# A two-layer decoder kernel: two masks leave the matmul engine

## The chip, the cores and the metric

One core of one Trainium2 chip runs the whole program. The metric is the time on the device of one execution in microseconds (us), the median of several runs. TensorE is called PE here, VectorE DVE, ScalarE ACT, GpSimd POOL, and SyncE, which issues most of the transfers, SP.

## The reference, cut to what matters

The sequence has 512 positions and the model 1024 channels. Two layers follow each other, each a token mixer and a gated MLP with a short causal convolution. The two mixers are what the change touches:

```python
# layer 0: stick-breaking attention, 16 heads of width 64, blocks of 128 queries
z = einsum('bqhd,bshd->bhqs', qb, k)              # qb holds the factor 1/8
strict = key_pos[None, :] < t[:, None]
log_keep = where(strict, log_sigmoid(-z), 0.0)
suffix = cumsum(log_keep, axis=3, reverse=True) - log_keep
a = where(strict, exp(log_sigmoid(z) + suffix), 0.0)

# layer 1: 16 heads of width 128 over one shared latent; the 128 keys of each query are chosen by an indexer
_, sel = top_k(isc, topk)                          # isc is NEG above the diagonal
logits = einsum('bqhd,bqkd->bqhk', qb, kg) * scale + bias(t - sel, head)
logits = where(valid, logits, NEG)                 # NEG = -1e30
p = softmax(logits)
```

In layer 0 a query sees only the keys before it, and its weight at key s is sigmoid(z[s]) times the product of sigmoid(-z) over the keys between s and t. In layer 1 the bias depends on the distance from query to key and on the head.

## The kernel before, in words

Activations lie transposed, 128 channels by 512 positions. Every dense product is made of three matmuls of rounded parts (`mm3`, lines 248 to 251): a matrix and its operand are each split in a high part (ACT, line 209 for weights) and a remainder (DVE, line 217). Weights come as chunks of 128x1024 fp32 through a pool `raws` of six buffers (line 126); `fetch` (191) keeps their loads, all on SP's queue, one chunk ahead of the splits in the program, and the queue itself runs ahead as far as buffers are free. The order of the instructions is written out by hand (`manual_schedule`): each engine executes its instructions in the order of the program text.

**Layer 0's attention** (`stick_layer`, lines 496 to 969). Each head has four query tiles j = 0 to 3 with (j+1)*128 keys. `scores` (846) makes z in PSUM by two matmuls (852, 853). A third one (854) multiplies an identity by the 128x128 matrix `strict_b`, which holds -1e30 on and above the diagonal, and adds it to the last 128 columns. ACT then writes m = sigmoid(-z/8) (861) and a = sigmoid(z/8) (862): masked places give m = 1 and a = 0. DVE runs a product over m from the right in place (866, `tensor_tensor_scan` with multiply and bypass) and multiplies a by the result shifted by one (867). PE transposes a (882), and `weighted` (894) multiplies it with the values (904). Between these, projections of later heads fill PE (`fill`, 837).

**Layer 1's attention** (`dsa_layer`, lines 1049 to 1498). The indexer leaves `maskb`, bf16, 0 or -1e30, 128x1280: the four query tiles side by side at columns LOFF = 0, 128, 384, 768. For a head h and a tile j, `logits` (1337) makes z by three matmuls (1343 to 1345) and a fourth one (1346), identity times the tile's part of `maskb`, that adds the mask. `softmax` (1348) scales z by the query's norm and adds the head's bias on DVE (1354), and takes the negative maximum (1356); `expo` (1358) is ACT's exponential with the row sums (1361). `transposed` (1365) turns the result on PE (1372) and copies it out of PSUM. There are two PSUM buffers for z, so a tile's logits wait until DVE has read the tile two before it. The bias lies in DRAM as one row per head (`rb`); `load_bias` (1325) loads it with a step of one element per partition, which makes a 128x512 table that all four tiles read backwards, into one of two buffers `th`.

Head 0's four tiles are made ahead of the loop (1436 to 1440). The loop (1448) over h then mixes the logits and softmax of head n = h+1 with the transposes of head h, the values of a pair of heads (1383, 1393), and steps of the last query projections and of the output projection (`fill`, 1319, whose `events` also hold the weight splits). At the end of an iteration it calls `load_bias(n + 1)` (1487), whose table is first read in the next iteration.

The lines that matter, with the line numbers of the profile:

Of the kernel before, what the change touches and what calls it, by code (L numbers as in the profile page):

```python
# [9 lines left out]
F32 = mybir.dt.float32  # L10
F32R = mybir.dt.float32r
BF = mybir.dt.bfloat16
AF = mybir.ActivationFunctionType
OP = mybir.AluOpType
# [4 lines left out]
D = 1024  # L19
S = 512  # L20
P = 128
KT = D // P
QT = S // P
# [4 lines left out]
HEADS = 16  # L28
# [4 lines left out]
NEG = -1e30  # L33
# [5 lines left out]
LATE_STEPS = [2, 3, 2, 3, 3, 3, 3, 3, 3, 3, 5, 5, 5, 5, 5, 8]  # L39
AHEAD = 2  # L40
FETCH = 1
IDXFILL = [1, 1, 1, 0, 1, 1, 1, 1]

TRP = [[(0, 0)], [(1, 0), (3, 384)], [(2, 0)]]
TRW = [512, 512, 256]
LOFF = [0, 128, 384, 768]
LW = 1280
TRO = [0, 512, 1024]

C_ID, C_STRICT, C_CAUSAL = 0, 128, 256  # L50
C_W = 384

S_ADAB, S_NM, S_NF, S_CW, S_CB = 0, 48, 56, 64, 64 + 132
S_L = 64 + 132 + 44
# [64 lines left out]
def kernel_body(ctx, tc, xT, wst, cst, smalls, crow, ccol, relb, onehot, outT):  # L119
    nc = tc.nc  # L120
# [16 lines left out]
    cons = cpool.tile([P, C_W], F32, name="cons")  # L137
    ident = cons[:, C_ID:C_ID + P]
    ident_b = cpool.tile([P, P], BF, name="ident_b")
    strict_b = cpool.tile([P, P], BF, name="strict_b")  # L140
    ones_mean = cpool.tile([P, P], F32, name="ones_mean")
    dve.memset(ones_mean, 1.0 / D)
    ecols = cpool.tile([P, 3], F32, name="ecols")
# [352 lines left out]
    def stick_layer(l):  # L496
        with ExitStack() as st:
# [233 lines left out]
                first_part(i, KT - 2)  # L731
            lo_part(KT - 1)
            dve.tensor_copy(ident_b, ident)
            dve.tensor_copy(strict_b, cons[:, C_STRICT:C_STRICT + P])
            V, O, QK, A_ = {}, {}, {}, {}
            kz = [[ap.tile([P, S], F32R, name=f"kz{b}{e}", bufs=1) for e in range(2)] for b in range(2)]
            for b in range(2):
# [108 lines left out]
            def scores(i, j):  # L846
                p, e = i // 2, i % 2
                q, kd, kl = QK[p][e], QK[p][2 + e], QK[p][4 + e]
                ns = (j + 1) * P
                z = ptile([P, S], "z", "z")  # L850
                qs = slice(j * P, ns)
                pe.matmul(z[:, :ns], lhsT=q[:, qs], rhs=kd[:, :ns], start=True, stop=False)
                pe.matmul(z[:, :ns], lhsT=q[:, qs], rhs=kl[:, :ns], start=False, stop=False)
                pe.matmul(z[:, qs], lhsT=ident_b, rhs=strict_b, start=False, stop=True)
                if j == 0:
                    A_[i] = ap.tile([P, LW], F32, name="a")
                a = A_[i][:, LOFF[j]:LOFF[j] + ns]

                def gates():
                    m = ap.tile([P, S], F32, name="m", bufs=2)  # L860
                    act.activation(m[:, :ns], z[:, :ns], AF.Sigmoid, scale=-0.125)
                    act.activation(a, z[:, :ns], AF.Sigmoid, scale=0.125)

                    def weights():
                        rev = m[:, :ns][:, ::-1]
                        dve.tensor_tensor_scan(rev, rev, rev, 1.0, OP.mult, OP.bypass)
                        dve.tensor_mul(a[:, :ns - 1], a[:, :ns - 1], m[:, 1:ns])

                    later(0.4, weights)

                later(0.2, gates)
                tick(0.1 * j + 0.15)
# [176 lines left out]
    def dsa_layer(l, first, man):  # L1049
        with ExitStack() as st:  # L1050
# [233 lines left out]
            with ExitStack() as sa:  # L1284
# [34 lines left out]
                def fill(n):  # L1319
                    for _ in range(n):  # L1320
                        next(filler, None)
                        if events:
                            events.pop(0)()

                def load_bias(h):
                    th = ths[h] = ap.tile([P, S], F32, name="th", bufs=2)
                    ov = rb[h:h + 1, 0:1]
                    nc.sync.dma_start(th, bass.AP(tensor=ov.tensor, offset=ov.offset, ap=[[1, P], [1, S]]))

                def begin(h):  # L1330
                    L = ap.tile([P, LW], F32, name="L")
# [5 lines left out]
                def logits(h, j):  # L1337
                    qh, ql = Q[h]
                    ns = (j + 1) * P
                    qs = slice(j * P, ns)  # L1340
                    ls = slice(LOFF[j], LOFF[j] + ns)
                    z = heads[h][4][j] = ptile([P, S], "z", "z")
                    pe.matmul(z[:, :ns], lhsT=qh[:, qs], rhs=kph[:, :ns], start=True, stop=False)
                    pe.matmul(z[:, :ns], lhsT=ql[:, qs], rhs=kph[:, :ns], start=False, stop=False)
                    pe.matmul(z[:, :ns], lhsT=qh[:, qs], rhs=kpl[:, :ns], start=False, stop=False)
                    pe.matmul(z[:, :ns], lhsT=ident_b, rhs=maskb[:, ls], start=False, stop=True)

                def softmax(h, j):
                    L, nm, sum_, rv, z = heads[h]
                    z = z.pop(j)  # L1350
                    ns = (j + 1) * P
                    ls = slice(LOFF[j], LOFF[j] + ns)
                    c = h * QT + j
                    dve.scalar_tensor_tensor(L[:, ls], z[:, :ns], rq[:, c:c + 1], ths[h][:, :ns][:, ::-1],
                                             op0=OP.mult, op1=OP.add)
                    dve.tensor_reduce(nm[:, j:j + 1], L[:, ls], axis=AX.X, op=OP.max, negate=True)

# [78 lines left out]
                for j in range(QT):  # L1436
                    logits(0, j)
                    fill(1)
                    softmax(0, j)
                    expo(0, j)  # L1440
                rvb = None

                def sums(h):
# [4 lines left out]
                for h in range(HEADS):  # L1448
                    n = h + 1
                    more = n < HEADS  # L1450
                    values = h % 2 == 0 and h > 0
                    if more:
                        begin(n)
                        for j in range(2):
                            logits(n, j)
                        softmax(n, 0)
                        expo(n, 0)
                    if values:
                        weighted(h - 2)
                    transposed(h, 0, True)  # L1460
                    if more:
                        softmax(n, 1)
                        expo(n, 1)
                    if h % 2 and h > 1:
                        pair_lo()
                    if not more:
                        rvb = sums(h)
                        pair_values(h - 1)
                    fill(LATE_STEPS[h] // 2)
                    if more:  # L1470
                        logits(n, 2)
                        softmax(n, 2)
                        expo(n, 2)
                    transposed(h, 1, False)
                    if values:
                        pair_scale(rvb)
                    if more:
                        rvb = sums(h)
                        logits(n, 3)
                    if h % 2 and more:  # L1480
                        pair_values(h - 1)
                    transposed(h, 2, True)
                    if more:
                        softmax(n, 3)
                        expo(n, 3)
                        if n + 1 < HEADS:
                            load_bias(n + 1)
                    else:
                        pair_scale(rvb)
                    fill(LATE_STEPS[h] - LATE_STEPS[h] // 2)  # L1490
                    if values:
                        pair_hi()
# [19 lines left out]
def _pack(i):  # L1512
# [13 lines left out]
    w = f["sb_w_in"][0]  # L1526
# [51 lines left out]
    cst = np.zeros((P, C_W), np.float32)  # L1578
    i = np.arange(P)
    cst[:, C_ID:C_ID + P] = np.eye(P)  # L1580
    cst[:, C_STRICT:C_STRICT + P] = np.where(i[None, :] < i[:, None], 0.0, NEG)
    cst[:, C_CAUSAL:C_CAUSAL + P] = np.where(i[None, :] <= i[:, None], 0.0, NEG)

    n = np.maximum(np.arange(640) - (P - 1), 0)
# [30 lines left out]
```

## Time and profile before

| | |
|---|---|
| time, median of 3 runs | 1299.84 us (1299.54 to 1299.88) |
| span of the profiled execution | 1297.7 us, 2.1 us below that median; the page names no other time for it |
| PE busy in the span | 1280.5 us (99%) |
| DVE, ACT, POOL busy | 930.7 (72%), 591.4 (46%), 35.8 us (3%) |
| layer 0's heads | about 57.8 to 237 us |
| layer 1's heads | about 763 to 902 us |
| mask matmuls of layer 0 (line 854) | 64, of 128x128 |
| mask matmuls of layer 1 (line 1346) | 64, of 128x128 to 128x512 |

The span runs from the first to the last instruction of one execution. "Busy" of PE is an upper bound of its work, since matmuls overlap and each row of a matmul also holds its way through the array: what a matmul costs is read from the distance between the starts of its neighbours. A chain is the sequence of work that ended last, followed back from the end. A line such as "A <- B: 21.9, 13, 3.3" says that A waited for B for 21.9 us in 13 places, at most 3.3 us in one.

### The profile page before, as it was taken

To read this page: it belongs to the slowest core of one execution; us is meant where nothing else is said; L and a number is where in the kernel's file an instruction comes from. 1 tells how busy PE (TensorE), PEld (TensorE's weight loads), DVE (VectorE), ACT (ScalarE), POOL (GpSimd) and SP (SyncE) were. 2 spreads that over 40 slices of the span, in tenths; PEclk is the share of its full clock that TensorE was granted. 3 is DMA by queue.
4 is the path that set the end of the run, shared out by engine and by line. 5 is a ranking of instruction groups with operands and counts; after the bars stand their busy time and mean duration, and the time that the engine had idled before them with its cause. 6 is when DMAs were issued, how large, how long until landed. Compare 5 with 4: busy or idle time off the path is not lost.

```text
span 1297.7 us, 18005 instructions
## 1 busy us (share of the span) xinstructions
PE 1280.5 (99%) x6988; PEld 1066.7 (82%) x6988; DVE 930.7 (72%) x1532; ACT 591.4 (46%) x1049; POOL 35.8 (3%) x27
## 2 busy tenths in 40 slices
PE   8999999999999999999999999999999999999998
PEld 5978787898888888888987777777998888888888
DVE  5888988778777877875778877777876456456643
ACT  5476666454323423442555346565554234234430
POOL 0000000000000000000102410000000000000000
PEclk9999999999999999999999999999999999999999
DMA  9644444324575575654213211213222422423221
GB/s 375 207 130 131 144 126 125 126 66 124 199 252 191 175 246 190 192 175 142 80 52 91 88 31 51 65 58 122 82 83 78 129 86 74 129 91 97 73 90 66
DMA packets 50613, 163.23 MB, mean 126 GB/s; under 512 B 5808, under 2 KB 8624, under 8 KB 50528
## 3 DMA queue, kind: packets, MB, share of 16 engines
q1 hardware_dynamic: 50096, 161.30, 38.6%
q8 instruction: 55, 0.90, 0.3%
q10 hardware_dynamic: 432, 0.79, 0.2%
q14 instruction: 30, 0.25, 0.1%
HBM read 159.92 MB, written 2.14 MB: 125 GB/s over the span
## 4 chain that ended last, share of the span: by engine, by line
PE 92%; DVE 3%; ACT 2%; DMA 1%; issue 1%; SPq 0%; DVEq 0%; ACTq 0%
PE pt_u L249 11%; PE pt_u L250 11%; PE pt_u L251 11%; PE pt_d L250 5%; PE pt_d L249 5%; PE pt_d L251 5%; PE pt_first L250 2%; PE pt_l L249 2%; PE pt_first L251 2%; PE pt_first L249 2%; PE pt_l L250 2%; PE pt_l L251 2%; PE pt_q L249 2%; PE pt_q L251 2%; PE pt_q L250 2%; PE pt_qk L249 2%
## 5 line engine op out<-in xcount | busy, mean ns | idle before, releaser
L209 ACT ACTIVATE whi<-raw 128x1024 fp32r<-128x1024 f32 (+1 forms) x206 | 205.2, 1002 | 118.8 <-PE pt_d L251 89.6
L249 PE MATMUL pt_u<-hhi,whi 128*128 128x512 f32 x640 | 249.4, 390 | 0.0
L250 PE MATMUL pt_u<-hhi,wlo 128*128 128x512 f32 x640 | 249.2, 389 | 0.0
L251 PE MATMUL pt_u<-hlo,whi 128*128 128x512 f32 x640 | 249.1, 389 | 0.0
L217 DVE TENSOR_TENSOR wlo<-raw,whi 128x1024 fp32r<-128x1024 f32 (+1 forms) x194 | 223.7, 1154 | 17.7 <-ACT whi L209 16.8
L985 ACT ACTIVATE y<-pt_u,sm 128x512 f32<-128x512 f32 x80 | 62.2, 777 | 188.3 <-PE pt_u L251 188.3
L249 PEld LDWEIGHTS pt_u<-hhi,whi 128*128 128x128 f32 x640 | 120.2, 188 | 26.0 <-issue 1.1
L251 PEld LDWEIGHTS pt_u<-hlo,whi 128*128 128x128 f32 x640 | 120.2, 188 | 24.9
L250 PEld LDWEIGHTS pt_u<-hhi,wlo 128*128 128x128 f32 x640 | 120.2, 188 | 24.7
L986 DVE SCALAR_TENSOR_TENSOR y<-pt_u,sm,y 128x511 f32<-128x511 f32 x80 | 59.9, 749 | 97.0 <-ACT y L985 96.8
L249 PE MATMUL pt_d<-acthi,whi 128*128 128x512 f32 x288 | 112.1, 389 | 0.0
L251 PE MATMUL pt_d<-actlo,whi 128*128 128x512 f32 x288 | 112.1, 389 | 0.0
L250 PE MATMUL pt_d<-acthi,wlo 128*128 128x512 f32 x288 | 112.1, 389 | 0.0
L258 DVE SCALAR_TENSOR_TENSOR raw<-raw,cond 128x1024 f32<-128x1024 f32 x88 | 106.6, 1217 | 3.8 <-DMA raw<-wst 3.8
L360 DVE SCALAR_TENSOR_TENSOR x<-pt_d,mod,x 128x512 f32<-128x512 f32 x48 | 36.0, 750 | 72.8 <-PE pt_d L251 72.8
L233 ACT ACTIVATE acthi<-y 128x512 fp32r<-128x512 f32 x44 | 27.8, 632 | 105.4 <-DVE y L1004 105.4
L249 PE MATMUL pt_first<-hhi,whi 128*128 128x256 f32 (+1 forms) x224 | 68.6, 306 | 0.1
L250 PE MATMUL pt_first<-hhi,wlo 128*128 128x256 f32 (+1 forms) x224 | 67.2, 300 | 0.9 <-DVE wlo L217 0.8
L251 PE MATMUL pt_first<-hlo,whi 128*128 128x256 f32 (+1 forms) x224 | 67.0, 299 | 0.0
L249 PEld LDWEIGHTS pt_d<-acthi,whi 128*128 128x128 f32 x288 | 54.1, 188 | 11.2
L251 PEld LDWEIGHTS pt_d<-actlo,whi 128*128 128x128 f32 x288 | 54.1, 188 | 11.2
L250 PEld LDWEIGHTS pt_d<-acthi,wlo 128*128 128x128 f32 x288 | 54.1, 188 | 11.2
(253 smaller groups left out, 2661.3 us busy)
## 6 DMA issues: line engine op xcount, KB each, us to landing
raw<-wst SPq DMA_DIRECT2D x250, 512.0 KB, 3.7
raw<-wst SPq DMA_DIRECT2D x48, 384.0 KB, 3.0
th<-rb SPq DMA_DIRECT2D x16, 256.0 KB, 3.5
ada<-wst SPq DMA_DIRECT2D x4, 512.0 KB, 6.3
outT<-x SPq DMA_DIRECT2D x16, 128.0 KB, 1.7
x<-xT SPq DMA_DIRECT2D x5, 256.0 KB, 5.0
x<-xT ACTq DMA_DIRECT2D x3, 256.0 KB, 3.9
cond<-crow SPq DMA_DIRECT2D x1, 512.0 KB, 10.5
```

The source lines that it names most:

```text
L209: act.activation(hi[:, :n], raw[:, :n], AF.Copy)
L217: engine.tensor_sub(lo[:, :n], raw[:, :n], hi[:, :n].bitcast(F32))
L233: act.activation(hi, src, AF.Copy)
L249: pe.matmul(out, lhsT=whi, rhs=ahi, start=start, stop=False)
L250: pe.matmul(out, lhsT=wlo, rhs=ahi, start=False, stop=False)
L251: pe.matmul(out, lhsT=whi, rhs=alo, start=False, stop=stop)
L258: dve.scalar_tensor_tensor(raw, raw, 1.0, cond, op0=OP.mult, op1=OP.mult, accum_out=dst)
L360: dve.scalar_tensor_tensor(x[f][:, c], pt, mod[l][:, g * KT + f:g * KT + f + 1], x[f][:, c], op0=OP.mult, op1=OP.add)
L985: act.activation(y, pt, AF.Identity, scale=cw[2], bias=sm[:, b + S_CB + c:b + S_CB + c + 1])
L986: dve.scalar_tensor_tensor(y[:, 1:], pt[:, :S - 1], cw[1], y[:, 1:], op0=OP.mult, op1=OP.add)
```

## The change

The matmuls of line 854 all go, and those of line 1346 for heads 2 to 15 (`PEMASK = 2`).

In layer 0 z is left unmasked. The scan runs over the columns 1 to the end of m, from the right, with start value 0 and with add as its second operation: the added operand is `below`, a table that holds a 1 in each row at the query's own key and 0 elsewhere. So the running product stays 0 above the diagonal, becomes 1 at it, and is the product of sigmoid(-z) below it. The last column of a, which has nothing to be multiplied with, is set to 0 by POOL.

In layer 1 ACT copies `maskb` once, backwards and as fp32, into two buffers of `raws`, and SP stores them to DRAM (`maskd`). For each head from 2 on `load_bias` now fills 128x1280 instead of 128x512, in two buffers of `raws`, by four loads on SP; then two transfers on POOL's queue read `maskd` and add it to what lies there (`accum_op`). Heads 0 and 1 load one table as before and keep their mask matmuls. The buffers `th` of their own are gone. `load_bias(n + 1)` moves from the end of the iteration to its start.

```diff
+PEMASK = 2
@@ stick_layer
-            dve.tensor_copy(strict_b, cons[:, C_STRICT:C_STRICT + P])
+            below = ap.tile([P, S], F32, name="below", bufs=1)
+            pool.memset(below, 0.0)
+            pool.tensor_copy(below[:, S - P - 1:S - 1], ident)
@@ scores
-                pe.matmul(z[:, :ns], lhsT=q[:, qs], rhs=kl[:, :ns], start=False, stop=False)
-                pe.matmul(z[:, qs], lhsT=ident_b, rhs=strict_b, start=False, stop=True)
+                pe.matmul(z[:, :ns], lhsT=q[:, qs], rhs=kl[:, :ns], start=False, stop=True)
...
-                    act.activation(a, z[:, :ns], AF.Sigmoid, scale=0.125)
+                    act.activation(a[:, :ns - 1], z[:, :ns - 1], AF.Sigmoid, scale=0.125)
+                    pool.memset(a[:, ns - 1:], 0.0)
...
-                        rev = m[:, :ns][:, ::-1]
-                        dve.tensor_tensor_scan(rev, rev, rev, 1.0, OP.mult, OP.bypass)
+                        rev = m[:, 1:ns][:, ::-1]
+                        dve.tensor_tensor_scan(rev, rev, below[:, S - ns:S - 1][:, ::-1], 0.0, OP.mult, OP.add)
@@ dsa_layer
+                maskd = dp.tile([P, LW], F32, name="maskd")
+                def halves_of():
+                    return [raws.tile([P, D], F32, name="th", tag="raw")[:, :w] for w in (LOFF[3], S)]
+                def store_mask():
+                    for t, c0 in zip(halves_of(), (0, LOFF[3])):
+                        for j in (0, 1, 2) if c0 == 0 else (3,):
+                            ns = (j + 1) * P
+                            act.activation(t[:, LOFF[j] - c0:LOFF[j] - c0 + ns], maskb[:, LOFF[j]:LOFF[j] + ns][:, ::-1], AF.Copy)
+                        nc.sync.dma_start(maskd[:, c0:c0 + t.shape[1]], t)
                 def load_bias(h):
-                    th = ths[h] = ap.tile([P, S], F32, name="th", bufs=2)
+                    th = ths[h] = halves_of() if h >= PEMASK else halves_of()[1:]
                     ov = rb[h:h + 1, 0:1]
-                    nc.sync.dma_start(th, bass.AP(tensor=ov.tensor, offset=ov.offset, ap=[[1, P], [1, S]]))
+                    for j in range(QT) if h >= PEMASK else (3,):
+                        ns = (j + 1) * P
+                        t = th[-1] if j == 3 else th[0][:, LOFF[j]:LOFF[j] + ns]
+                        nc.sync.dma_start(t, bass.AP(tensor=ov.tensor, offset=ov.offset, ap=[[1, P], [1, ns]]))
+                    if h >= PEMASK:
+                        pool.dma_start(th[0], maskd[:, :LOFF[3]], accum_op=OP.add)
+                        pool.dma_start(th[1], maskd[:, LOFF[3]:], accum_op=OP.add)
@@ logits
-                    pe.matmul(z[:, :ns], lhsT=ident_b, rhs=maskb[:, ls], start=False, stop=True)
+                    if h < PEMASK:
+                        pe.matmul(z[:, :ns], lhsT=ident_b, rhs=maskb[:, ls], start=False, stop=True)
@@ after head 0's four tiles
+                store_mask()
@@ loop over h, n = h + 1
+                    if n + 1 < HEADS:
+                        load_bias(n + 1)
                     if more:
                         begin(n)
...
                         softmax(n, 3)
                         expo(n, 3)
-                        if n + 1 < HEADS:
-                            load_bias(n + 1)
```

`softmax` takes its second operand from `bias_of(h, j)`, the tile's part of the new tables, read backwards as before. The constants lose `strict`'s 128 columns.

More of the change, by code (lines that the diff above doesn't have):

```diff
@@ L48 @@
 TRO = [0, 512, 1024]
-C_ID, C_STRICT, C_CAUSAL = 0, 128, 256
-C_W = 384
+C_ID, C_CAUSAL = 0, 128
+C_W = 256
 S_ADAB, S_NM, S_NF, S_CW, S_CB = 0, 48, 56, 64, 64 + 132
@@ L139, in kernel_body @@
     ident_b = cpool.tile([P, P], BF, name="ident_b")
-    strict_b = cpool.tile([P, P], BF, name="strict_b")
     ones_mean = cpool.tile([P, P], F32, name="ones_mean")
@@ L1323, in fill, with bias_of @@
                             events.pop(0)()
+                maskd = dp.tile([P, LW], F32, name="maskd")
[7 more added lines that the diff above has]
+                        nc.sync.dma_start(maskd[:, c0:c0 + t.shape[1]], t)
                 def load_bias(h):
-                    th = ths[h] = ap.tile([P, S], F32, name="th", bufs=2)
+                    th = ths[h] = halves_of() if h >= PEMASK else halves_of()[1:]
                     ov = rb[h:h + 1, 0:1]
-                    nc.sync.dma_start(th, bass.AP(tensor=ov.tensor, offset=ov.offset, ap=[[1, P], [1, S]]))
+                    for j in range(QT) if h >= PEMASK else (3,):
[5 more added lines that the diff above has]
+                        pool.dma_start(th[1], maskd[:, LOFF[3]:], accum_op=OP.add)
+                def bias_of(h, j):
+                    ns = (j + 1) * P
+                    if j == 3 or h < PEMASK:
+                        return ths[h][-1][:, :ns][:, ::-1]
+                    return ths[h][0][:, LOFF[j]:LOFF[j] + ns][:, ::-1]
                 def begin(h):
@@ L1344, in logits @@
                     pe.matmul(z[:, :ns], lhsT=ql[:, qs], rhs=kph[:, :ns], start=False, stop=False)
-                    pe.matmul(z[:, :ns], lhsT=qh[:, qs], rhs=kpl[:, :ns], start=False, stop=False)
-                    pe.matmul(z[:, :ns], lhsT=ident_b, rhs=maskb[:, ls], start=False, stop=True)
+                    pe.matmul(z[:, :ns], lhsT=qh[:, qs], rhs=kpl[:, :ns], start=False, stop=h >= PEMASK)
+                    if h < PEMASK:
+                        pe.matmul(z[:, :ns], lhsT=ident_b, rhs=maskb[:, ls], start=False, stop=True)
                 def softmax(h, j):
@@ L1353, in softmax @@
                     c = h * QT + j
-                    dve.scalar_tensor_tensor(L[:, ls], z[:, :ns], rq[:, c:c + 1], ths[h][:, :ns][:, ::-1],
+                    dve.scalar_tensor_tensor(L[:, ls], z[:, :ns], rq[:, c:c + 1], bias_of(h, j),
                                              op0=OP.mult, op1=OP.add)
@@ L1580, in _pack @@
     cst[:, C_ID:C_ID + P] = np.eye(P)
-    cst[:, C_STRICT:C_STRICT + P] = np.where(i[None, :] < i[:, None], 0.0, NEG)
     cst[:, C_CAUSAL:C_CAUSAL + P] = np.where(i[None, :] <= i[:, None], 0.0, NEG)
```

## The prediction

> **What bounds the kernel now.** I read the page first, then the busy time of the two stretches that the change touches, then their waits and chains, and last their timelines.
>
> ```profile
> PE 1280.5 (99%) x6988; PEld 1066.7 (82%) x6988; DVE 930.7 (72%) x1532; ACT 591.4 (46%) x1049; POOL 35.8 (3%) x27
> ...
> PE 92%; DVE 3%; ACT 2%; DMA 1%; issue 1%; SPq 0%; DVEq 0%; ACTq 0%
> ```
>
> PE carries 92% of the chain that ends last. So a matmul that goes is worth about what it costs, where nothing else is waiting beside it. That has to be asked of each stretch (columns: stretch, length, busy time and count of each engine, granted clock):
>
> ```profile
> core 0 of [0], span 1297.7 us
> core 0: us, PE busy (x) PEld busy (x) DVE busy (x) ACT busy (x) POOL busy (x), PEclk, DMA share, GB/s
> 57.80:237.00 179.20, 179.06 (x1107) 143.75 (x1106) 159.65 (x238) 120.88 (x254) 0.00 (x0) 1.00 0.42 133
> 763.00:902.00 139.00, 134.80 (x851) 104.13 (x851) 102.43 (x209) 81.96 (x218) 0.00 (x0) 1.00 0.23 73
> ```
>
> In layer 0's heads PE has no idle time (179.06 of 179.20), but DVE is close behind with 159.65. In layer 1's heads PE and DVE pass work to each other: DVE has 36.6 us to spare, and PE is held up a little. The waits of that stretch and its chain show both directions:
>
> ```profile
> DVE L L1354 <- PE z L1346: 21.9, 13, 3.3
> ...
> PEld z L1343 <- DVE L L1354: 4.1, 3, 1.8
> ...
> by line: PE av L1404 12.8%; PE tr L1372 9.3%; DVE L L1354 6.2%; PE z L1343 5.8%; DVE nm L1356 5.4%; PE z L1344 5.1%; PE z L1345 5.0%; PE z L1346 4.9%; PE pv L1387 4.5%; PE pt_o L249 4.1%; PE pt_o L251 4.0%; PE pt_o L250 3.9%; PE pt_q L251 3
> ```
>
> DVE waits for the mask matmul itself for 21.9 us, PE for DVE's reading of z for 4.1 us. The mask matmul carries 4.9% of that chain.
>
> **Layer 0, the matmuls.** Starts are what counts:
>
> ```profile
> 182.53 0.28 PE L853 MATMUL z<-kz,qs 128*128 128x256 f32 x1
> 182.65 0.23 PE L854 MATMUL z<-strict_b,ident_b 128*128 128x128 bf16 x1
> 182.69 0.37 PE L249 MATMUL pt_v<-whi,hhi 128*128 128x256 f32 x1
> 182.90 0.28 PE L250 MATMUL pt_v<-whi,hlo 128*128 128x256 f32 x1
> 183.02 0.28 PE L251 MATMUL pt_v<-wlo,hhi 128*128 128x256 f32 x1
> ...
> 185.35 0.23 PE L854 MATMUL z<-strict_b,ident_b 128*128 128x128 bf16 x1
> 185.42 0.61 PE L882 MATMUL tr<-cons,a 128*128 128x128 f32 x4
> ```
>
> A 256-column matmul takes 0.12 us (182.90 to 183.02). Without the mask L249 would start at 182.65 and L250 at 182.77; it starts at 182.90. The mask costs 0.13: 0.04 itself, and the rest because the short one doesn't cover the next weight load. The first mask of a head is alike. The third and fourth stand ahead of transposes and cost 0.07 each. A head: 0.13 + 0.13 + 0.07 + 0.07 = 0.40, sixteen heads 6.4 us. DVE has 19.5 us idle here, which after the change would be 13; I take 6.0, with 4 and 6.4 as ends.
>
> **Layer 0, what is added.** The scan keeps its count and loses one column of each:
>
> ```profile
> L866 DVE TENSOR_TENSOR_SCAN m<-m 128x512 f32<-128x512 f32 x16 | 19.5, 1220 | 0.0
> ```
>
> 1220 ns for 512 columns is 2.4 ns a column, so it is already slower than DVE's plain passes; it reads two operands now as before, and only the second operation differs. I take no change; the other end is a rival below. POOL's 64 one-column memsets fall on an engine that is idle in the whole stretch (0.00 above) and need only be done before the transposes an iteration later; if they were late, PE would wait at line 882. `below` takes one memset and one copy ahead of the other memsets on POOL's queue; they wait for the constants, whose load was issued long before the first head. The cast of `strict_b` was not on the chain. All of these: 0.
>
> **Layer 1, the matmuls.**
>
> ```profile
> 843.93 0.34 PE L1346 MATMUL z<-maskb,ident_b 128*128 128x384 bf16 x1
> 844.10 0.60 PE L1372 MATMUL tr<-cons,L 128*128 128x128 f32 x4
> ...
> 845.24 0.39 PE L1346 MATMUL z<-maskb,ident_b 128*128 128x512 bf16 x1
> 845.47 1.05 PE L1387 MATMUL pv<-uvc,latf 128*128 128x128 f32 x8
> ```
>
> 0.17 us for 384 columns and 0.23 for 512; by columns 0.12 for 256; the one of 128 costs 0.12 as in layer 0, for the same reason. A head: 0.64, fourteen heads 9.0 us of PE. How much of that is kept? The chain gives the lower end: 4.9% of 139 us is 6.8 us for sixteen heads, 6.0 for fourteen. The upper end is all 9.0. Since DVE also gets z earlier, I take 7.0.
>
> **Layer 1, how the biases arrive.** Here is the price. Each table now needs its buffers, four loads on SP, and then an adding transfer that waits for them. The rows nearest to these:
>
> ```profile
> raw<-wst SPq DMA_DIRECT2D x250, 512.0 KB, 3.7
> raw<-wst SPq DMA_DIRECT2D x48, 384.0 KB, 3.0
> th<-rb SPq DMA_DIRECT2D x16, 256.0 KB, 3.5
> ...
> L1328 SPq DMA_DIRECT2D th<-rb x16: 319/320/431, 763.6 to 875.8; - x16
> ```
>
> An issue takes 0.32 us and a load lands after about 3.5. Three loads must land for the first three tiles: 3 x 0.32 + 3.5 = 4.5 us. No row shows an adding transfer or one from POOL. Call the time from its issue to its landing A. Its lower end is the plain 384 KB transfer, 3.0. It reads two operands and writes one, so an upper end is three plain ones in a row, 9.0. I take 4.5, one and a half plain ones: 512 KB take only 0.7 longer than 384, so most of the 3.0 is not the bytes, and the second operand should not cost it again in full. The Trainium skill (DMA: Bandwidth & Descriptors, section "Anatomy of one DMA — SWDGE (gpsimd) path") has a fit of 2.0 us plus the bytes over 436 GB/s for a plain transfer from GpSimd, which makes 2.9 us of 384 KB, as estimated from that page; with A at 2.9 the time forecast below would be 1289.2 instead of 1290.8, and no run yet shows it.
>
> *In the steady state* the question is whether a table is there in time. Its buffers come from the six of `raws`, of which two tables take four and the weights one or two; the one it waits for is at worst that of the table two heads back, freed when DVE has read its third tile. The shortest such distance in the trace is head 7 to head 9:
>
> ```profile
> 820.87 0.62 DVE L1354 SCALAR_TENSOR_TENSOR L<-z,cols,th 128x384 f32<-128x384 f32 x1 [3.31 <-PE z L1346]
> ...
> 833.38 0.34 DVE L1354 SCALAR_TENSOR_TENSOR L<-z,cols,th 128x128 f32<-128x128 f32 x1
> ```
>
> From 821.5 to 833.4 are 11.9 us, some 10.9 when each of two heads is half a microsecond shorter. 4.5 + A = 9.0 is less: covered with 1.9 us to spare. The two heads' transfers follow each other on POOL's queue, where nothing else stands (0.00 again). SP has three issues a head more, 1.0 us of the 8.7 that a head takes (139.0 over 16), but it mostly stands waiting:
>
> ```profile
> SPq L1328 <- DVE L L1354: 101.5, 14, 9.1
> ```
>
> That wait for a buffer was ahead of the weight loads before too, and moving `load_bias` to the front of the iteration changes only its place among loads that are needed heads later. Cost 0; without that cover, a late weight chunk would hold ACT at line 209.
>
> *At head 2* it is not covered. The mask must first be copied, stored and landed:
>
> ```profile
> 771.29 0.72 ACT L1361 ACTIVATE L<-L,nm 128x512 f32<-128x512 f32 x1 [1.16 <-DVE nm L1356]
> ...
> 777.69 0.34 DVE L1354 SCALAR_TENSOR_TENSOR L<-z,cols,th 128x128 f32<-128x128 f32 x1
> ...
> 779.75 0.42 PE L1343 MATMUL z<-kph,qh 128*128 128x384 f32 x1
> ```
>
> The first line is head 0's last exponential. Behind it ACT makes the four copies, at most 0.72 each, by their widths about 1.2 for the first three: 773.3. The store is issued, and takes 3.0 by the row of its size: 776.5. Then SP issues the other store and head 2's loads (they need no wait for the first): landed about 778.3. The adding transfer lands at 778.3 + 4.5 = 782.8. DVE reads it at 777.69 before: it now stands for 5.1 us, and behind it on DVE wait the other tiles, the copy of the transposes and the weight split. PE goes on until head 2's third tile needs the z buffer (779.75, about 779.5 without two masks) and starts it at 783.2: 3.7 lost, and some more while DVE works off its queue: 4.0. In general A - 0.5. ACT's copies put head 1's exponentials back by 1.9 us; they disappear in that wait. Head 3's table comes before the late head 2 lets it be read.
>
> **The sum**, against the profiled execution: 1297.7 - 6.0 - 7.0 + 4.0 = 1288.7 us of span. The median of the runs is 2.1 above the span: 1290.8 us. About 0.2% (2.6 us) is what a measurement of this kernel can tell from no change: faster is below 1297.2, slower above 1302.4.
>
> **The rivals.** *The biases come late at every head (slower).* Place: DVE's line 1354 of a head's first tile. It decides from 4.5 + A above 10.9, that is from A = 6.4. Each further microsecond costs 1.0 at head 2 and, shared by the two heads of a cycle, 0.5 at each of thirteen heads at most; where a table gets a buffer that has been free for longer, nothing. At A = 8 that is 7.5 + 0.8 x 13 = 18 at most and some 13 if a half of the heads are spared, and the gain of 13 is gone. At A = 9: 8.5 + 17 at most, some 20, and 1299.8 - 13 + 20 = about 1307. For it: no row shows such a transfer, and it moves the 384 KB twice and through an engine that issues nothing now. Against it: plain transfers of this size and even larger ones land in 3.0 to 3.7 in this trace. 0.15.
>
> *DVE takes PE's place in layer 0.* If DVE's 19.5 us idle there are waits that can't be moved, the stretch keeps its 179.2 us: 1296.8. For it: 89% busy, in an order written by hand. Against: PE shows no wait for DVE in it. 0.10.
>
> *The clock falls at head 2.* The granted clock is 1.00 in both stretches, but there PE's longest wait for z is 1.8 us, not 3.7. If after it PE ran at half its speed for as long as it stood, that would cost 1.9: 1292.7. The Trainium skill (TensorE: Matmul & The Clock Gate, Part 1) says that the clock halves after an idle window of about 3.4 us, and comes back after as much busy time; by the page's figure the estimate is 1.7. 0.10.
>
> *The scan's second operation makes it half as slow again.* If that is a half of the 2.4 ns, 1280 columns of sixteen heads make 25 us more of DVE, more than its 19.5 idle: layer 0's heads take 185 at least and with a half of the present waits some 195, and the time is about 1290.8 + 6 + 16 = 1313. Against it: the row above has nothing to set the two operations apart, and a scan without second operation is already slow. 0.03.
>
> **How the numbers follow.** The forecast of 1290.8 has 0.62. Its own range goes from A = 3 and all of the matmuls (-15.4 + 2.5: 1286.9) to the low ends and A = 6.4 (-10 + 5.9: 1295.7). Low is 1286. High has to take in the DVE rival and a part of the first rival; at 1303 some 0.13 is left out above and some 0.05 below. Faster: 0.62 + 0.10 (clock) and half of the DVE rival, less a little for A between 6 and 8: 0.73. Slower: most of the first rival and the scan: 0.16. Same: 0.11.
>
> **What would show it.** No rows of line 854, eight of line 1346 (heads 0 and 1). Scans of 511 columns still near 1220 ns. Layer 0's stretch 6 us shorter with PE still without idle time; layer 1's about 3 shorter, with one long wait of DVE's bias line for POOL's transfer, some 5 us, at head 2, and PE waiting for z behind it, and none of either after it. The issues row of the adding transfers gives A directly: with A over 6.4 and waits at many heads the first rival holds; with a shorter first stretch missing, the second.

## The result, and the profile after

| | before | after |
|---|---|---|
| median, runs beside each other | 1299.69 us (1299.38 to 1299.88, 4 runs) | 1308.28 us (1305.59 to 1310.32, 4 runs) |
| ratio | | 1.0065 (95%: 1.005 to 1.0079) |
| span of the profiled execution | 1297.7 us | 1303.8 us (its time: 1305.59) |
| layer 1's heads, first logits to last values | 763.2 to 902.4: 139.2 us | 757.5 to 908.4: 150.9 us |

The kernel became 8.6 us slower; the forecast was 9 us faster. The two halves of the change went opposite ways: layer 1's heads begin 5.7 us earlier, as forecast, and then take 11.7 us more instead of 3 less.

In the changed kernel the scan is line 868, the loads of the bias 1346, the adding transfers 1348 and 1349, the logits 1370 to 1372, the bias on DVE 1382, its maximum 1384. From its page, the granted clock in 40 slices and the chain that ended last:

```profile
PEclk9999999999999999999999989999999999999999
...
PE 87%; DVE 5%; DMA 3%; ACT 2%; issue 2%; SPq 0%; another core or an unknown queue 0%; DVEq 0%; ACTq 0%; POOLq 0%
```

PE carries 87% of the chain instead of 92, DVE and the transfers 8% instead of 4, and the clock has one slice below full. The same two stretches as in the prediction (the columns end with clock, busy share of the DMA engines, GB/s):

```profile
57.80:237.00 179.20, 178.39 (x1069) 147.00 (x1068) 163.78 (x245) 121.80 (x255) 2.89 (x56) 1.00 0.42 138
763.00:902.00 139.00, 119.98 (x725) 95.38 (x723) 94.40 (x192) 75.94 (x205) 24.45 (x28) 0.94 0.86 172
```

Layer 0 is still full of PE. In layer 1 PE stands still for 19.0 us of the same window instead of 4.2, and the DMA engines went from 0.23 to 0.86 busy. The scan, from the groups of layer 0's stretch:

```profile
L868 DVE TENSOR_TENSOR_SCAN m<-m,below 128x511 f32<-128x511 f32 x16 | 19.5, 1218 | 0.0
```

1218 ns for 511 columns against 1220 for 512: its second operation costs nothing here. The waits of layer 1's stretch (total, times, longest) name the late work, and the transfers' rows there (count, size, median us from issue to landing; above them packets, MB and share of 16 engines) show how busy the transfers are:

```profile
PEld z L1370 <- DVE L L1382: 18.8, 9, 10.3
DVE L L1382 <- DMA th<-maskd: 18.6, 4, 11.9
PE z L1370 <- DVE L L1382: 16.0, 6, 10.2
```

```profile
q1 hardware_dynamic: 9663, 14.61, 46.8%
q0 software_dynamic: 4032, 9.18, 38.4%
...
th<-maskd POOLq DMA_DIRECT2D x14, 384.0 KB, 6.8
...
th<-maskd POOLq DMA_DIRECT2D x14, 256.0 KB, 6.7
th<-rb SPq DMA_DIRECT2D x14, 192.0 KB, 6.7
```

The adds (queue q0) land after 6.8 us, and the loads, of which the largest took 3.5 us before, after 6.7. Head 2, in the timeline:

```profile
769.77 0.68 DVE L1086 TENSOR_TENSOR ql<-pt_q,qh 128x512 fp32r<-128x512 f32 x1
...
775.49 1.01 POOL L1348 DMA_DIRECT2D th<-maskd  x1 [22.98 <-DMA th<-rb]
...
782.38 0.35 DVE L1382 SCALAR_TENSOR_TENSOR L<-z,cols,th 128x128 f32<-128x128 f32 x1 [11.93 <-DMA th<-maskd]
...
782.79 0.69 PE L1370 MATMUL z<-kph,qh 128*128 128x384 f32 x1 [10.22 <-DVE L L1382]
```

DVE is idle from 770.45, POOL issues the add only when the loads have landed, 6.9 us later DVE goes on, and PE has stood still for 10.2 us. Later, DVE waits at heads 6, 7, 9, 10 and 15, by 1.4 to 3.3 us each:

```profile
816.11 0.35 DVE L1382 SCALAR_TENSOR_TENSOR L<-z,cols,th 128x128 f32<-128x128 f32 x1 [3.30 <-issue]
...
843.14 0.35 DVE L1382 SCALAR_TENSOR_TENSOR L<-z,cols,th 128x128 f32<-128x128 f32 x1 [3.11 <-DMA th<-maskd]
```

### The profile page after: what moved, and what is told of

Its sections match the earlier page's. It is cut to its first block, busy times and chain, and to the rows that moved or that the text cites. A ratio compares the mean times of both kernels' runs of the same rounds, so it can differ in the third digit from the quotient of the medians.

```text
span 1303.8 us, 18041 instructions
## 1 busy us (share of the span) xinstructions
PE 1271.7 (98%) x6867; PEld 1066.2 (82%) x6868; DVE 929.8 (71%) x1531; ACT 592.5 (45%) x1053; POOL 64.3 (5%) x121
## 3 DMA queue, kind: packets, MB, share of 16 engines
q0 software_dynamic: 4032, 9.18, 4.1%
## 4 chain that ended last, share of the span: by engine, by line
PE 87%; DVE 5%; DMA 3%; ACT 2%; issue 2%; SPq 0%; another core or an unknown queue 0%; DVEq 0%; ACTq 0%; POOLq 0%
PE pt_u L249 11%; PE pt_u L251 11%; PE pt_u L250 11%; PE pt_d L251 5%; PE pt_d L250 5%; PE pt_d L249 5%; PE pt_first L249 2%; PE pt_first L251 2%; PE pt_first L250 2%; PE pt_q L249 2%; PE pt_q L251 2%; PE pt_q L250 2%; PE pt_l L250 2%; PE pt_l L249 2%; PE pt_l L251 2%
## 5 line engine op out<-in xcount | busy, mean ns | idle before, releaser
L250 PEld LDWEIGHTS pt_d<-acthi,wlo 128*128 128x128 f32 x288 | 54.1, 188 | 11.3
```

Of the source, the lines that this page charges most:

```text
L250: pe.matmul(out, lhsT=wlo, rhs=ahi, start=False, stop=False)
```

## The experiments

The theory after the result: a bias is now two transfers behind each other, and each is longer beside the other than alone; so it comes late, once badly at head 2 and a little at many heads. Rivals: the buffers and loads are at fault and not the adds; the adding as such; the fall of the clock; harm from the stick layer's part. In all comparisons the kernel before, run beside the experiments, had medians of 1299.7 to 1299.9 us.

**The stick layer's part alone.** The diff of `stick_layer` and `scores` stays, that of `dsa_layer` is undone:

```diff
-                    th = ths[h] = halves_of() if h >= PEMASK else halves_of()[1:]
+                    th = ths[h] = ap.tile([P, S], F32, name="th", bufs=2)
...
+                    pe.matmul(z[:, :ns], lhsT=ident_b, rhs=maskb[:, ls], start=False, stop=True)
```

> The stick layer's part of the change alone; the second attention is that of the kernel before, its mask matmuls and its one load per head included. The theory (the first part gains what its matmuls took, the whole loss lies in the second attention): in the changed kernel the first logits of layer 1 start at 757.5 us instead of 763.2, so 1299.7 - 5.7 = 1294.0 us, and layer 1's heads again take 139 us. Rival (the stick part does harm further on, since POOL's memsets, the new table or another placing of buffers cost something there): 1297 us or more, or layer 1's heads longer than 141 us.

Measured: 1294.22 us (1293.80 to 1295.93), ratio 0.9959 (0.9945 to 0.9973); layer 1's heads from 758.0 to 897.1, 139.1 us. The first part is worth 5.7 us and harms nothing. All of the loss lies in layer 1.

**The adding transfers left out.**

```diff
-                    if h >= PEMASK:
-                        pool.dma_start(th[0], maskd[:, :LOFF[3]], accum_op=OP.add)
-                        pool.dma_start(th[1], maskd[:, LOFF[3]:], accum_op=OP.add)
```

> The changed kernel without the adding transfers, so that heads 2 to 15 are computed without the mask; the store, the four loads per head and the buffers stay. The theory (the adding transfers, by their length and by the bandwidth that they take from the loads, make the biases late): no wait for a bias left, loads land in about 3.0 to 4 us again, layer 1's heads take 139.2 - 7 = 132 us and the time is 1300 - 5.7 - 7 = 1287 us. Rival (the buffers taken from the pool of the weight chunks and four loads per head on SP's queue make them late, and the adds only come on top): waits for the loads stay at heads 2, 6, 7, 9, layer 1's heads take 139 us or more, 1294 us or more.

Measured: 1289.23 us (1288.95 to 1290.61), ratio 0.9918 (0.9903 to 0.9933); layer 1's heads 758.2 to 891.8, 133.6 us. From its waits and transfers:

```profile
DVE L L1379 <- DMA th<-rb: 1.7, 2, 1.0
```

```profile
q1 hardware_dynamic: 10224, 16.65, 55.0%
...
th<-rb SPq DMA_DIRECT2D x14, 192.0 KB, 5.4
```

No bias is late by more than 1.0 us. So buffers from the chunks' pool and four loads per head are not at fault by themselves, though the loads land in 5.4 us and not in the 3.0 to 4 expected: with no add in flight four loads beside each other already take longer than one did. Against the stick part alone, fourteen heads of mask matmuls give 5.0 us (5.5 in the profiled stretch, 0.39 a head), less than the 7 forecast. The adds then cost 1308.28 - 1289.23 = 19.1 us, where 4.0 were forecast. This sum holds a change of waits, too: without the add, a head's first tile waits for the load of its own 128 columns alone (64 KB). At head 2 DVE reads it at 772.12, when that load has landed (772.02) and the 192 KB one hasn't (775.00). The first add waits for all three.

**Mask matmuls kept to head 3.**

```diff
-PEMASK = 2
+PEMASK = 4
```

> The changed kernel with the mask matmuls kept for heads 0 to 3 instead of 0 and 1: the first adding transfers now belong to head 4, after a pause in which the mask has long been stored. The theory (late biases, in two parts: a chain store, loads, adds ahead of head 2 that costs 10.4 us against the kernel before, and later heads whose loads and adds crowd the transfer engines): the wait of 11.9 us at head 2 goes, two more heads of mask matmuls cost 2 x 0.6 us, so about 1308.3 - 10 = 1298 to 1300 us if the chain of the first adding head was a matter of the store just ahead of it, with waits of 1 to 3 us left at some later heads. Rival (the chain only moves: the first adding head is late wherever it is): a wait of 10 us or more at head 4, and 1306 to 1309 us.

Measured: 1298.34 us (1293.53 to 1300.62, 10 runs), ratio 0.9983 (0.9971 to 0.9994). The profiled execution was the quickest of the ten, 1293.53; in it

```profile
DVE L L1382 <- DMA th<-maskd: 7.2, 3, 4.1
```

remains, at later heads, and none at head 4. With two more heads of matmuls at 0.4 us each, head 2's chain costs 1308.28 - 1298.34 + 0.8 = 10.7 us and the later heads 1298.34 - 0.8 - 1289.23 = 8.3: together the 19. This split rests on medians. In the profiled execution the later heads cost 1293.53 - 0.8 - 1289.23 = 3.5 us, at a mean granted clock of 1.000; the nine longer ones list 0.994 to 0.997. So a part of the 8.3 goes with falls of the clock; how large it is stays open, as none of the nine was profiled.

**Small adds, and adds aside.** Both start from the kernel with mask matmuls to head 3. In the first an add takes 64 KB instead of 384 and 256; in the second it has its size, but nobody waits for it:

```diff
-                        pool.dma_start(th[0], maskd[:, :LOFF[3]], accum_op=OP.add)
+                        pool.dma_start(th[0][:, :P], maskd[:, :P], accum_op=OP.add)
```

```diff
-                        pool.dma_start(th[0], maskd[:, :LOFF[3]], accum_op=OP.add)
+                        pool.dma_start(aside[:, :LOFF[3]], maskd[:, :LOFF[3]], accum_op=OP.add)
```

> The kernel with mask matmuls for heads 0 to 3, whose adding transfers take only the first 128 columns of each buffer (64 KB each instead of 384 and 256), so that most of the mask is missing for heads 4 to 15. Loads, order, waits and the number of transfers stay; 80% of the added bytes go. Theory (the bytes of loads and adds together crowd the transfer engines): the adds land in 3 us or less, the loads in 5 us or less, no bias is late, and the time is that without adds plus two heads of mask matmuls, 1289.2 + 0.8 = 1290 us. Rival (a second transfer behind the first is too late whatever its size): 1295 to 1298 us, with waits for it as in the kernel with full adds.

> The same kernel whose adding transfers have their full size (32 of the last 512 columns are left out for want of room) but add to a buffer of their own that nobody reads, so that heads 4 to 15 are computed without the mask. The bytes flow beside the loads as before, each pair as soon as the pair before it has landed, about 769 to 860 us; no bias waits for an add. Theory in its strong form (the adds' bytes alone slow the loads so that these come late): waits for the loads, 1295 us or more. In its weaker form (the bytes lengthen every landing, but only the sum of load and add behind each other, about 6 + 7 us, is more than the 11 us that a bias has): loads land in about 6 us as in the kernel with adds, and yet 1290 to 1292 us.

Measured: 1289.70 us (1288.04 to 1290.55), ratio 0.9915 (0.9899 to 0.9932), with small adds; 1288.71 (1288.26 to 1288.85), ratio 0.991 (0.9896 to 0.9925), with adds aside. Transfers of the first, then of the second:

```profile
th<-rb SPq DMA_DIRECT2D x12, 192.0 KB, 5.5
...
th<-maskd POOLq DMA_DIRECT2D x24, 64.0 KB, 4.0
th<-rb SPq DMA_DIRECT2D x12, 64.0 KB, 3.5
```

```profile
q0 software_dynamic: 3456, 7.67, 31.4%
...
aside<-maskd POOLq DMA_DIRECT2D x12, 384.0 KB, 7.6
...
th<-rb SPq DMA_DIRECT2D x12, 192.0 KB, 7.0
...
th<-rb SPq DMA_DIRECT2D x12, 64.0 KB, 5.2
```

Full adds beside the loads are harmless as long as no bias waits for them, though the loads then take 7.0 us. With small adds the time is as expected, with landing times of 4.0 and 5.5 us above the 3 and 5 expected, but the edit did more than its text says. A small add covers tile 0's columns alone, so it waits for the 64 KB load and no longer for three loads. Head 6 shows it: its loads are issued from 790.15 us on and land 3.5, 4.5 and 5.4 us after their issues, and its first add is issued at 794.22, ahead of the second landing. So this run shortens the chain twice, by the bytes and by the waits, and doesn't tell them apart. Nor was no bias late: head 7's small add, issued at 802.32, landed after 9.8 us, and DVE waited there:

```profile
DVE L L1382 <- DMA th<-maskd: 3.9, 1, 3.9
```

What tile 0's bias needs is, by medians, the 64 KB load alone; that load and the small add; or two issues (at a median of 0.42 us in the changed kernel) ahead of the 192 KB load, that load, and the full add. The prediction has 10.9 us from a free buffer to its use:

| kernel | until tile 0's bias is there | median |
|---|---|---|
| adds aside | 5.2 us | 1288.7 us |
| small adds | 3.5 + 4.0 = 7.5 | 1289.7 |
| full adds, mask matmuls to head 3 | 0.8 + 6.4 + 6.6 = 13.8 | 1298.3 |

The traces, read head by head, agree. From the issue of a head's first load to the landing of its first add pass 15.2 us in the median in the changed kernel (12.2 to 18.8), 14.9 with mask matmuls to head 3, and 8.6 with small adds. The room can be read from the kernel without adds: from head 4 on DVE reads a head's bias 10.1 (head 7) to 18.6 us after the issue of its first load. The five heads behind head 2 that wait in the changed kernel, 6, 7, 9, 10 and 15, have 12.4, 10.1, 11.9, 14.1 and 12.5 us there, all less than 15.2. Heads 4 and 12, with 11.5 and 13.7, met shorter chains (12.8 and 13.6) and waited 0.2 us at most. So full adds behind three loads are too late where the room is short, and the shorter chains mostly are not.

The strong form of the theory, that the bytes alone make the loads late, fell; the weaker one named 1290 to 1292 us, and 1288.7 came.

**Plain transfers in place of adding ones.** The mask overwrites the bias, with the same sizes and waits:

```diff
-                        pool.dma_start(th[0], maskd[:, :LOFF[3]], accum_op=OP.add)
+                        pool.dma_start(th[0], maskd[:, :LOFF[3]])
```

> The changed kernel whose transfers on POOL's queue overwrite the buffers with the mask instead of adding it, so that heads 2 to 15 have the mask and no bias; sizes, order and waits are the same. If it is the adding that makes these transfers long and fills the transfer engines: they land in about 3.5 to 5 us instead of 6.7, the busy share of the engines falls well under the 0.86 of the changed kernel, the wait at head 2 shrinks by 2 to 3 us, and the time comes to about 1295 to 1301 us. Rival (it is the bytes and the order, load first and then a second transfer, and adding costs nothing of its own): landing times of 6 to 7 us, and 1305 to 1310 us as changed.

Measured: 1304.35 us (1301.97 to 1306.06), ratio 1.0033 (1.0023 to 1.0043).

```profile
q0 software_dynamic: 2240, 9.18, 19.8%
...
th<-maskd POOLq DMA_DIRECT2D x14, 384.0 KB, 4.5
...
th<-rb SPq DMA_DIRECT2D x14, 192.0 KB, 6.0
```

The same 9.18 MB take half of the engines' time and land 2.3 us sooner, as expected; the time is not, 1295 to 1301 us were expected. The adding as such is worth 4 of the 19 us. Head 2 still waits 11.1 us, not 2 to 3 less: its first transfer is issued at 776.0, when its loads have landed, and lands after 6.5 us, though it adds nothing. By the sum of the table the chain is here 0.8 + 6.0 + 4.5 = 11.3 us, and behind head 3 DVE waits for these transfers at two heads (7 and 9, 6.5 and 1.3 us) instead of five.

**Store and head 2 ahead of head 0.**

```diff
                 load_bias(1)
+                store_mask()
+                load_bias(2)
                 begin(0)
```

> The changed kernel with the store of the mask and the loads and adds of head 2 moved ahead of head 0's tiles, behind the loads of heads 0 and 1. The theory (the wait of 11.9 us at head 2 is the chain of store, loads and add that begins too late): that wait goes and the time falls to that of the kernel with mask matmuls up to head 3, plus nothing for the two heads, so about 1298 us, less 1 us if ACT's five copies ahead of head 0's exponentials cost nothing. Rival (the first adding head is slowed by its transfers whatever the order): a wait of 5 us or more stays at head 2, 1303 us or more.

Measured: 1302.98 us over ten runs, ratio 1.0031 (1.0013 to 1.005). Nine runs lie between 1299.48 and 1309.00, with a median of 1301.95; the tenth took 1799.33 at a granted clock of 0.654, which nothing here explains, and the ratio leaves it out. In the profiled execution, the quickest, the wait at head 2 shrinks from 11.9 to 7.1 us because its add is issued at 770.77 instead of 775.49:

```profile
770.77 1.01 POOL L1348 DMA_DIRECT2D th<-maskd  x1 [17.50 <-DMA th<-rb]
```

The theory missed: the wait did not go. The rival's wait of 5 us or more stayed, at a time that lies close to its 1303. Some 6 us, a little over half of the chain's price, go. On SP's queue the loads still stand behind the store, which waits for ACT's copies, and from their issue at 763.98 to the bias at 778.33 it is 14.3 us, against 14.6 in the changed kernel (767.79 to 782.38): the chain begins earlier and is as long.

**The clock at head 2, twice.** More matmuls whose result nobody reads, for the time of PE's wait; first into a buffer of the values' ring, then into that of head 1's transposes:

```diff
+                            pe.matmul(idle, lhsT=ident_b, rhs=maskb[:, LOFF[3]:], start=True, stop=True)
```

> The changed kernel with 38 more matmuls of 128x512 (identity times a part of the mask, into a PSUM buffer that nobody reads) where PE waits at head 2, about 9 us of work in a wait of 10.2 us. The theory that the fall of the granted clock there (0.50 from 774 to 786 us, 0.81 to 788) takes about 2 us of PE's time: the clock stays at 1.00 in this stretch and the time falls by about 2 us, to 1306 us. Rival (the clock's fall costs nothing, since the bias of the next tiles is late anyway): 1308 us as changed.

> The changed kernel with 36 more matmuls of 128x512 (identity times a part of the mask) into the PSUM buffer of head 1's first transposes, ahead of these, so that they wait for nothing that is late: 8.5 us of work for PE ahead of a wait of 10.2 us, which leaves 2 us of it. Theory that the clock's fall at head 2 takes about 2 us of PE's time there: the clock stays near 1.00 at 774 to 788 us and the time falls to about 1306 us. If it costs nothing: 1308 us; if the additional work gets in the way: more.

The first missed its aim: 1316.45 us (1315.51 to 1317.57), ratio 1.0126 (1.0111 to 1.0141). Its matmuls waited for a buffer whose reader on ACT is held up by the same late bias, and ran behind the wait:

```profile
785.61 0.58 PE L1504 MATMUL idle<-maskb,ident_b 128*128 128x512 bf16 x1 [12.43 <-ACT cols L1095]
786.41 9.55 PE L1504 MATMUL idle<-maskb,ident_b 128*128 128x512 bf16 x36 [0.22 <-issue]
795.61 0.53 PE L1370 MATMUL z<-kph,qh 128*128 128x384 f32 x1
...
798.35 0.38 PE L1400 MATMUL tr<-cons,L 128*128 128x128 f32 x2
```

It shows something all the same. From head 2's third tile to the last transposes PE takes 2.74 us here (795.61 to 798.35), after the clock is back; in the changed kernel the same instructions take 4.49 us:

```profile
782.79 0.69 PE L1370 MATMUL z<-kph,qh 128*128 128x384 f32 x1 [10.22 <-DVE L L1382]
...
787.28 0.38 PE L1400 MATMUL tr<-cons,L 128*128 128x128 f32 x2
```

```profile
784.00:786.00 2.00, 2.00 (x8) 1.76 (x7) 1.97 (x3) 0.68 (x4) 0.00 (x0) 0.50 0.98 175
786.00:788.00 2.00, 2.00 (x14) 1.86 (x13) 1.93 (x6) 1.23 (x4) 0.00 (x0) 0.81 0.60 61
```

That is 1.75 us more, with a granted clock of 0.50 and, at the end, 0.81. The second try gave 1305.85 us (1304.55 to 1307.77), ratio 1.0044 (1.0029 to 1.0059). Its matmuls run from 771.8 to 779.6 at full clock, but 3.4 us of waiting remain behind them and the clock falls to 0.54 at 786 to 788 us all the same. Its runs overlap with those of the changed kernel, so it proves nothing about the 2 us.

**POOL adds by arithmetic.** One 128x512 load per head as before, no store, no adding transfer:

```diff
-                        pool.dma_start(th[0], maskd[:, :LOFF[3]], accum_op=OP.add)
+                        pool.tensor_tensor(out=t, in0=th[:, :ns][:, ::-1], in1=maskb[:, LOFF[j]:LOFF[j] + ns], op=OP.add)
```

> The mask is added to the bias by POOL's own arithmetic instead of transfers: one 128x512 load per head into two buffers as in the kernel before, then four additions per head from 2 on, each of the reversed bias and the mask (bf16) into the two buffers from the pool of weight chunks; no store of the mask, no transfer that adds. POOL is busy 5% of the span, and 1280 columns at DVE's rate for two operands (693 ns for 511) would be 1.7 us per head, twice or three times that if POOL is slower; there are 9 us per head. The theory (the adds as transfers are what is wrong, the removal of the matmuls is worth what was forecast): about 1300 - 5.7 - 7 = 1287 us, no wait at head 2. Rival (buffers from the pool of weight chunks are late anyway, or POOL's additions slow DVE's two-operand work down): 1294 us or more, with DVE's rows longer or with waits for the sums.

Measured: 1291.07 us (1290.13 to 1292.13), ratio 0.993 (0.9915 to 0.9945): it beats both kernels, but falls between the 1287 of the theory and the 1294 of the rival. Against the stick part alone it gains 3.2 us, where the kernel without adds gains 5.0. Its groups on POOL, and DVE's wait for a transfer:

```profile
L1340 POOL TENSOR_TENSOR sum<-th,maskb 128x512 f32<-128x512 f32 x14 | 16.6, 1186 | 13.6 <-DVE L L1368 13.6
...
L1340 POOL TENSOR_TENSOR sum<-th,maskb 128x128 f32<-128x128 f32 x14 | 6.2, 444 | 59.4 <-DVE L L1368 20.0 <-PE z L1360 15.7 <-DVE wlo L217 14.8
```

```profile
DVE L L1368 <- DMA th<-rb: 1.7, 1, 1.7
```

The four additions of a head take 3.2 us, and no sum is late. Two variants gain nothing more:

```diff
-                        pool.tensor_tensor(out=t, in0=th[:, :ns][:, ::-1], in1=maskb[:, LOFF[j]:LOFF[j] + ns], op=OP.add)
+                        pool.tensor_tensor(out=L[:, ls], in0=ths[h][:, :ns][:, ::-1], in1=maskb[:, ls], op=OP.add)
```

> POOL adds bias and mask as in the kernel with POOL's additions, but into the buffer L that softmax then updates in place, so that no buffer of the weight chunks is used; loads as in the kernel before. The theory (with the transfers gone the matmuls' time comes back in full): 1288 to 1290 us, no wait for the sums longer than 1 us. Rival (L is free too late, since it is held until the transposes of the head two before, and POOL's additions of 3.2 us per head stand in the path of the first tile): a DVE wait of 1 us or more at every head, 1295 us or more.

```diff
-PEMASK = 2
+PEMASK = 0
```

> The kernel whose mask is added by POOL's arithmetic into buffers of the weight chunks (1291.1 us), now for heads 0 and 1 too: no mask matmul is left. Eight matmuls fewer are worth 2 x 0.4 us by what the other heads gave: 1290.3 us. If the additions for head 0, which can only begin once the indexer's mask is there, stand in the path of its first tiles (0.44 to 1.19 us each): 1291 to 1293 us.

Measured: 1293.04 us (1291.01 to 1293.68), ratio 0.9943 (0.9928 to 0.9958), for sums in L; no wait for them, so the rival's reason is out, but the time was missed by 3 us, for a reason that stays open. For all heads 1292.17 us (1290.00 to 1292.61), ratio 0.9934 (0.9919 to 0.9949), with one wait of 2.2 us for POOL at head 0, as the second half of its expectation has it.

## Why the prediction was wrong

**Layer 0** was right: 6.0 forecast, 5.7 measured, the scan unchanged, POOL's memsets hidden. The rivals of DVE in PE's place and of a slow scan are out.

**Layer 1's matmuls** were mis-sized: 7.0 with ends of 6.0 and 9.0, measured 5.0 to 5.5. A part is the price of a mask matmul. From the start of a tile's first logits matmul to the next work on PE, the medians fall from 0.33, 0.62, 0.71 and 1.01 us (stick part alone, heads 2 to 15) to 0.30, 0.48, 0.54 and 0.78 (no adds). That is 0.57 a head and not 0.64, because the one of 128 columns costs 0.03 here and not 0.12 as in layer 0. Fourteen heads make 8.0 us of it. PE's idle time in the stretch rises from 4.7 to 5.6 us; where the rest of the distance to 5.5 goes stays open. The prediction also reads DVE's 21.9 us as waiting for the mask matmul itself; it waits for z, whichever matmul ends it, and without the mask still for 15.0 us.

**The step that failed** is the cover in the steady state: "4.5 + A = 9.0 is less: covered with 1.9 us to spare", which made the cost at later heads 0. Both terms were priced from plain transfers as they landed in the kernel before, each by itself. The three loads were to take 4.5 us. Without any add the 192 KB load alone already lands after 5.4, since four loads go out where one went, and with the adds after 6.7. The add was to take 4.5 and took 6.8; the same bytes without adding took 4.5. So the chain is 0.8 + 6.7 + 6.8 = 14.3 us by medians, and 15.2 head by head, where 9.0 was forecast; the room of 10.9 was about right (10.1 to 14.1 at the five heads that wait).

The change brings 640 KB of loads and 640 KB of adds per head where there were 256, and the engines' share goes from 0.23 to 0.55 with the loads alone and to 0.86 with the adds. The 0.23 stood in the same row that the prediction quoted, and the bytes were in the diff; they were never put together. That adds lengthen the loads is shown (5.4 to 6.7 and 7.0); that the loads lengthen the adds is not, as no run has adds without loads.

The 2.9 us that the prediction worked out by the Trainium skill (DMA: Bandwidth & Descriptors, "Anatomy of one DMA — SWDGE (gpsimd) path") were for a plain transfer. Here plain ones of 384 KB landed in 3.3 us at the least and 4.5 in the median, and no add of that size in less than 4.6; the measurement decides.

**The first rival** therefore happened, and its point was met: it was to decide from A above 6.4, and A came to 6.8. Yet its price list at 6.8 would have been 6.3 us at head 2 and 0.4 x 0.5 x 13 = 2.6 later, too little to cancel the gain. It too held the load at 4.5. With a load of 6.7 the sum is 14.3 us, 3.4 over 10.9; at most 0.5 x 3.4 x 13 = 22 us, and 8.3 were paid by the medians. Five of the thirteen later heads waited, as the reservation on buffers that are free for longer allowed.

**Head 2**: PE loses 10.2 us instead of 3.7. With all times 5.7 earlier the forecast had the add issued at 772.6; it was issued at 775.5, since the third load landed 6.2 us after its issue and not 3.5 (5.9 without any add, so the adds are not the reason; head 3's four loads follow it at once, which argues for crowding but isn't shown); it took 6.9 instead of 4.5; and DVE stood ready at 770.45, 1.5 earlier than reckoned. These make 2.9 + 2.4 + 1.5 = 6.8 us, and DVE's wait is 11.9 instead of 5.1.

**The clock rival** happened as well, 1.75 us by the rows above against 1.9 forecast. It followed the long wait and was not an outcome beside the others. That the sizes meet is luck: the rival lets PE run slowly for as long as it stood, which for 10.2 us would cost 5.1. The prediction's other estimate, 1.7, does not hang on the length of the wait, and it is the one that the rows bear out. The fall also came a second time: behind a pause of PE of 2.4 us at head 6 the clock is 0.87, 0.50 and 0.77 in the three stretches of 2 us from 816 us on, at most 2 x (0.13 + 0.50 + 0.23) = 1.7 us more, which neither the forecast nor the rival has.

The sum: -5.7 - 5.0 + 10.7 + 8.3 = +8.3, against +8.4 from the median shown before to the one after. It closes because its terms are differences of the same medians, and proves nothing by that; the forecast had -6.0 - 7.0 + 4.0 + 0.

## What to carry to other kernels

Before a transfer is priced from a row of the same kernel, add up the bytes and the rows that the change puts on the engines per iteration, and read the busy share of the DMA engines in that stretch: a landing time holds only for the load that it was measured under. The rows count too. From the kernel before to the one without adds, the bytes in the row of the hardware queue rise 1.7 times (9.96 to 16.65 MB), the packets 2.6 times (3888 to 10224) and the share 2.4 times (23.0% to 55.0%). Two transfers behind each other for one operand are the case to fear, since the operand waits for the sum, and the second waits for every load that its range covers. In this kernel the small sum of two operands in SBUF was better done by an idle engine's arithmetic: one load of 256 KB and 3.2 us of POOL per head were in time, where 1280 KB of transfers were not.

## What the hardware showed that was not expected

An adding transfer takes about twice the engines' time of a plain one of the same bytes: 9.18 MB took 38.4% of sixteen engines in the changed kernel and 19.8% when they overwrote, with 4032 and 2240 packets. Over the 139 us of the stretch that makes 0.21 and 0.20 us a packet on average: the plain ones take fewer packets, hardly quicker ones. POOL's issue took 0.86 us and 0.54.

The clock can fall without a long idle time. In the changed kernel a pause of 2.4 us was enough (at 816 us, above). In the kernel with POOL's additions it was 1.00 up to 842 us and then

```profile
842.00:844.00 2.00, 2.00 (x6) 0.59 (x8) 1.03 (x2) 1.95 (x5) 1.10 (x3) 0.54 0.00 0
844.00:846.00 2.00, 2.00 (x13) 1.01 (x10) 1.88 (x6) 1.15 (x2) 0.82 (x1) 0.61 0.00 0
```

while PE's longest pause in the 5 us before was 0.70 us (838.75 to 839.45), ahead of eight matmuls of one column (839.45, 1.05 us). By the clocks of the two rows that costs 2 x 0.46 + 2 x 0.39 = 1.7 us, nearly the distance from that kernel to the one without adds (1.8 us); that the two are the same was not tried. The Trainium skill (TensorE: Matmul & The Clock Gate, Part 1) puts the fall after an idle window of about 3.4 us; the 10.2 us at head 2 agree with it, these rows don't.
